# A chunked delta-rule recurrence: two pairs of small matmul groups issued alternately, and output heads in exchanged partition halves

## The chip, the cores and the metric

The kernel runs on one core of one Trainium2 chip. The metric is the device time of one execution in microseconds (us). Engines are named as in the profile: PE is TensorE (matmul), DVE is VectorE, ACT is ScalarE, POOL is GpSimd, SP issues DMAs.

## The reference

The model is a trunk of two layers over 1024 tokens of width 1024, in float32. Layer 0 mixes with a gated MLP and a pooling, layer 1 with the RWKV-7 time mixing; each is followed by a SwiGLU feed-forward part. The change touches the time mixing of layer 1 alone. Its core is this recurrence over tokens, for 16 heads with a state of 64 x 64 each:

```
def step(state, inp):
    r_t, w_t, k_t, v_t, a_t, b_t = inp
    sa = jnp.einsum('bhvk,bhk->bhv', state, a_t)
    state = (state * w_t[:, :, None, :] + sa[..., None] * b_t[:, :, None, :]
             + v_t[..., None] * k_t[:, :, None, :])
    return state, jnp.einsum('bhvk,bhk->bhv', state, r_t)
...
mean = jnp.mean(y, axis=-1, keepdims=True)
var = jnp.mean(jnp.square(y - mean), axis=-1, keepdims=True)
y = ((y - mean) * lax.rsqrt(var + GN_EPS)).reshape(bsz, seq, d)
y = y * ln_w.astype(f32) + ln_b.astype(f32)
bonus = jnp.sum(rh * kh * r_k.astype(f32), axis=-1, keepdims=True) * vh
y = (y + bonus.reshape(bsz, seq, d)).astype(h.dtype)
return (y * g) @ w_o, v_first
```

The kernel does not step token by token. It takes chunks of 64 tokens and solves each chunk with matrix products: with decayed a, b, k, r it forms all products inside the chunk, inverts a unit triangular 64 x 64 matrix, and carries the state only from chunk to chunk.

## The kernel before

The 1024 tokens are processed in two halves of 512, so there are eight chunks in each half and sixteen in all. Earlier stages write what a chunk needs to DRAM: `ar_d` (decayed a and r), `bk_d` (b and k), `v_d`, and `xi_d` (inverses of the 32 x 32 diagonal blocks of the triangular matrix). The function `recur` then runs the chunks of a half. It is a generator: `drive` interleaves its steps with those of a dense feed-forward stream (`ffn`), whose products are 128 x 128 x 512 and fill TensorE. The numbers that the generators yield are weights for that interleaving: small ones (0.1) inside a burst, and `BURST` = 12.0 between bursts.

Sixteen heads lie as eight pairs `p` with two members `r`: member r of a pair has its 64 rows in partitions 0 to 63 (r = 0) or 64 to 127 (r = 1). A product of 64 x 64 so uses one quarter of the 128 x 128 array: the operands' partition half picks the rows, the result's partition half picks the columns. All small products go through the helper `mm` (line 1460 is the call that the profile names for each), which chains them in program order with `issue_after`; dense products are placed between them by the tile planner, which simulates a timeline and gives the recurrence's instructions a priority ahead of the dense ones.

One chunk is one `burst` (line 1561), which issues, in this order:

- `below2` (line 1537): the lower left block of the inverse, 16 products of 32 x 32, copied into `XT` by ScalarE (r = 0) and VectorE (r = 1);
- `own` (line 1550): ov = the chunk's own values through its strictly lower products, copied from PSUM by ScalarE into `akv`. Its products read one partition half and write the other;
- oq: the state seen through a (`ar[..., 0, :]` with `S0`), products that read and write the same half; VectorE adds `akv` and oq into `Q` (line 1570);
- `gram` of the next chunk, first half: 16 products over all four quarters, masked from PSUM into `gt` by two VectorE multiplications (line 1507);
- ou: the solve, the inverse `XT` applied to `Q`; copied into `uv` by ScalarE (half 0, line 1577) and VectorE (half 1, line 1578);
- the output's state term (line 1587): r (`ar[..., 1, :]`) with `S0` into the PSUM tile `yp`;
- `gram` of the next chunk, second half; the state update (line 1597) with two VectorE operations; the output's own term, added into `yp` (line 1606); then `flip_bk` (transposes of the next chunk's b and k), loads by DMA for the chunk after next, and `below` (line 1521).

`yp` has two banks of PSUM, one per chunk of a pair of chunks. After the second chunk of a pair `post` (line 1632) copies both into `ysb` with ScalarE, normalises each head (VectorE, GpSimd), applies the weight `lnw`, adds the bonus term (`vch` times `bon`), and leaves `turn_out` (line 1678) to transpose the result and multiply it by the gate during the next burst. `lnw`, `vch` and `bon` are loaded by DMAs on SP's queue.

PSUM has eight banks. In these stages (`MIXED`, line 391) three go to the dense products, three to the small products (`sm`), two to `yp`.

Of the kernel before, what the change touches and what calls it, by code (L numbers as in the profile page):

```python
# [16 lines left out]
P = 128  # L17
# [26 lines left out]
def tile_trunk(  # L44
# [346 lines left out]
    MIXED = {"mm": ("mm", 3), "aux": ("sm", 3), "sm": ("sm", 3)}  # L391
# [792 lines left out]
    def project(h, hn1, kp, ring, keep, before_v):  # L1184
# [181 lines left out]
        for r in range(2):  # L1366
            sp.dma_start(
                bon[rows[r], h * 8 : h * 8 + 8, :], bon_d[h][:, :, r, :].rearrange("j (c t) p -> t (j c) p", t=64)
            )
# [70 lines left out]
    def recur(h, wp, stream):  # L1440
# [12 lines left out]
        C, ypair, loaded = {}, {}, [None]  # L1453
# [41 lines left out]
        def gram(c, q):  # L1495
            ar, bk, _, gt, _, _ = C[c]
            og = [pst("sm").rearrange("p (a b) -> p a b", b=P) for _ in range(2)]
            for j in range(4):
                p = q * 4 + j
                for b in range(2):  # L1500
                    for r in range(2):
                        mm(
                            og[r][rows[b], j, :], bk[rows[r], p, b, :],
                            ar[rows[r], p].rearrange("p a b -> p (a b)"), start=True, stop=True,
                        )
# [31 lines left out]
        def below2(c, w1):  # L1537
            XT = C[c][5]
            ox = smt()
            for p in range(8):  # L1540
                for r in range(2):
# [8 lines left out]
        def own(c):  # L1550

            _, _, uv, gt, _, _ = C[c]
            ov = smt()
# [3 lines left out]
            akv = wt("akv", 1, [P, 8, 64])  # L1557
            act.activation(akv, ov, AF.Copy)
            return akv

        def burst(c, bkt, w1):
# [4 lines left out]
            akv = own(c)  # L1566
            oq = smt()
            each(oq, lambda r, p: ar[rows[r], p, 0, :], lambda r, p: S0[rows[r], p, :])
            Q = wt("Q", 1, [P, 8, 64])
            dve.tensor_tensor(out=Q, in0=akv, in1=oq, op=ALU.add)  # L1570
# [5 lines left out]
            each(ou, lambda r, p: XT[rows[r], p, :], lambda r, p: Q[rows[r], p, :])  # L1576
            act.activation(uv[rows[0], 0], ou[rows[0]], AF.Copy)
            dve.tensor_copy(uv[rows[1], 1], ou[rows[1]])
            yield 0.1
            if c % 2 == 0:  # L1580
                ypair[0] = psum["pool"].tile([P, 2, 8, 64], F32, tag="y", bufs=1, name="yp")

            yp = ypair[0][:, c % 2]
            for p in range(8):
                for r in range(2):
                    mm(
                        yp[rows[r], p, :], ar[rows[r], p, 1, :], S0[rows[r], p, :], start=p == 0, stop=False,
                        skip_group_check=True,
                    )
# [13 lines left out]
            for p in range(8):  # L1603
                for r in range(2):
                    mm(
                        yp[rows[r], p, :], gt[:, p, r, 64:128], uv[:, r, p, :], start=False, stop=p == 7,
                        skip_group_check=True,
                    )
            C.pop(c)
            yield 0.1  # L1610
            if more:
# [5 lines left out]
                if c == 0:  # L1617
                    with tc.issue_after(loaded[0].ins):
                        for r in range(2):
                            i = sp.dma_start(  # L1620
                                lnw[rows[r]],
# [10 lines left out]
        def post(jj):  # L1632
            ysb = wt("ysb", 1, [P, 2, 8, 64])
            for r in range(2):
                act.activation(ysb[:, r], ypair[0][:, r], AF.Copy)
# [3 lines left out]
            with tc.issue_after(loaded[1].ins):  # L1639
                sp.dma_start(gch, g_d[h][:, :, jj * P : (jj + 1) * P])  # L1640
                for r in range(2):
                    sp.dma_start(
                        vch[rows[r]].rearrange("t c p d -> t c (p d)"),
# [6 lines left out]
            for r in range(2):  # L1650
                for p in range(8):
                    dve.bn_stats(out=st[:, r, p, :], in_=ysb[:, r, p, :])
# [13 lines left out]
            for p in range(8):  # L1666
                act.activation(
                    ysb[:, 1, p, :], ysb[:, 1, p, :], AF.Identity, scale=var[:, 8 + p : 9 + p], bias=mean[:, 8 + p : 9 + p]
                )
            dve.tensor_tensor(out=ysb[:, 0], in0=ysb[:, 0], in1=vb, op=ALU.mult)  # L1670
            dve.tensor_tensor(out=ysb[:, 0], in0=ysb[:, 0], in1=mb, op=ALU.add)
            yield 0.3
            for q in range(2):
                dve.tensor_tensor(out=ysb[:, q], in0=ysb[:, q], in1=lnw, op=ALU.mult)
                dve.tensor_tensor(out=ysb[:, q], in0=ysb[:, q], in1=vch[:, q], op=ALU.add)
            yield 0.3

            def turn_out():
                for q in range(2):
                    o = pst("sm")  # L1680
                    for i in range(4):
# [3 lines left out]
                            ysb[:, i % 2, p : p + 2, :].rearrange("t p d -> t (p d)"), ident,  # L1685
                        )
                    ov = o.rearrange("p (q c r t) -> p q r c t", q=2, c=2, r=2)
                    for i in range(4):
# [3 lines left out]
                            out=g, in0=ov[:, i // 2, i % 2], scalar=col(C_LNB + m), in1=g, op0=ALU.add, op1=ALU.mult,  # L1692
# [345 lines left out]
```

## Time and profile before

| | us |
|---|---|
| median of 3 timed runs (lowest 2453.6, highest 2456.31) | 2454.44 |
| span of the profiled execution | 2450.8 |
| first small product of the recurrence, first half | 1060.5 |
| last, second half (a transpose of `turn_out`) | 1834.4 |

The profiled execution's own time is known by its span alone, first to last instruction; the timed runs include what lies around it. In the views below a line gives the start in us, the duration, the engine, the line of the kernel, the operation, what it writes and reads by the program's tile names, the shape, and how many were merged (x); in brackets stands how long the engine was idle before and what released it. A view of waits gives us in total, times, and the longest. A stretch gives for each engine busy us and instructions, then the granted clock, the DMA engines' share and GB/s.

### The profile page before, as it was taken

The page shows a single profiled execution, that of the slowest core. Times are in us where ns is not written, and L with a number is a line of the kernel's source. Part 1 is how long each engine was busy: PE and PEld are TensorE (multiplying, and loading weights), DVE is VectorE, ACT ScalarE, POOL GpSimd, SP SyncE. Part 2 cuts the span into 40 slices and gives each one's busy share as a digit, 9 for nine tenths or more (in the row PEclk, how much of TensorE's full clock was granted, in tenths as well). Part 3 has the DMA queues.
Part 4 walks back from the last instruction along what each step waited for, and adds up shares of the span by engine and source line. Part 5 has one row for each costly group of instructions (what it writes and reads, how often), then busy time and mean ns, then how long its engine had stood idle before and what let it go on. Part 6 is the DMA issues. An engine that isn't in the chain of part 4 may idle for free. (4 is left out here: it accounts for less than half of the span.)

```text
span 2450.8 us, 38190 instructions
## 1 busy us (share of the span) xinstructions
PE 2369.0 (97%) x15567; PEld 1945.9 (79%) x15567; DVE 1476.8 (60%) x2328; ACT 935.9 (38%) x1403; POOL 217.1 (9%) x246
## 2 busy tenths in 40 slices
PE   8999999999899999999999999999999999999998
PEld 6888888888687788778777678777888788888887
DVE  6445766655558758856767947856664446434443
ACT  6233444443114644422335744433232324322223
POOL 0200000000000033101100133201100001000001
PEclk9999999999999999999999999999999999999999
DMA  5114443334655554774435465675433422433231
GB/s 177 52 60 140 153 146 103 113 103 155 252 203 204 165 149 131 226 212 132 129 126 155 160 166 141 186 223 158 143 112 122 129 78 90 150 105 95 86 103 52
DMA packets 406767, 342.17 MB, mean 140 GB/s; under 512 B 78080, under 2 KB 351616, under 8 KB 405824
## 3 DMA queue, kind: packets, MB, share of 16 engines
q10 hardware_dynamic: 266048, 195.33, 26.3%
q1 hardware_dynamic: 140544, 144.41, 18.8%
q8 instruction: 122, 2.00, 0.3%
q14 instruction: 53, 0.43, 0.0%
HBM read 263.07 MB, written 76.61 MB: 139 GB/s over the span
## 5 line engine op out<-in xcount | busy, mean ns | idle before, releaser
L399 PE MATMUL mm<-ahi,whi 128*128 128x512 f32 x1376 | 541.0, 394 | 5.8 <-DVE h L493 3.7
L400 PE MATMUL mm<-alo,whi 128*128 128x512 f32 x1376 | 541.5, 394 | 1.1 <-DVE alo L158 1.1
L401 PE MATMUL mm<-ahi,wlo 128*128 128x512 f32 x1376 | 540.1, 393 | 1.4 <-DVE wlo L158 1.4
L157 ACT ACTIVATE whi<-raw 128x1024 fp32r<-128x1024 f32 (+1 forms) x280 | 282.0, 1013 | 557.4 <-PE mm L400 428.6
L158 DVE TENSOR_TENSOR wlo<-raw,whi 128x1024 fp32r<-128x1024 f32 (+1 forms) x280 | 328.4, 1177 | 246.5 <-ACT whi L157 231.0
L399 PEld LDWEIGHTS mm<-ahi,whi 128*128 128x128 f32 x1376 | 259.0, 188 | 63.1 <-ACT whi L157 6.2
L401 PEld LDWEIGHTS mm<-ahi,wlo 128*128 128x128 f32 x1376 | 259.2, 188 | 58.4 <-DVE wlo L158 2.7
L400 PEld LDWEIGHTS mm<-alo,whi 128*128 128x128 f32 x1376 | 259.3, 188 | 57.7 <-issue 2.5
L493 DVE TENSOR_TENSOR h<-h,mm 128x512 f32<-128x512 f32 x276 | 185.5, 684 | 162.5 <-PE mm L401 161.6
L399 PE MATMUL mm<-hidhi,wdhi 128*128 128x512 f32 x304 | 117.5, 395 | 2.9 <-ACT hidhi L958 2.3
L400 PE MATMUL mm<-hidlo,wdhi 128*128 128x512 f32 x304 | 119.7, 394 | 0.0
L401 PE MATMUL mm<-hidhi,wdlo 128*128 128x512 f32 x304 | 119.0, 391 | 0.0
L730 PE MATMUL mm<-ahi,whi 128*128 128x512 f32 x296 | 115.6, 390 | 0.0
L731 PE MATMUL mm<-alo,whi 128*128 128x512 f32 x296 | 115.2, 389 | 0.0
L732 PE MATMUL mm<-ahi,wlo 128*128 128x512 f32 x296 | 113.6, 389 | 0.0
L157 ACT ACTIVATE wdhi<-raw 128x1024 fp32r<-128x1024 f32 x42 | 43.5, 1058 | 168.0 <-PE mm L400 133.1
L955 DVE TENSOR_TENSOR sg<-sg,mm 128x512 f32<-128x512 f32 x52 | 35.7, 687 | 118.9 <-PE mm L401 118.7
L399 PE MATMUL mm<-hd,dhi 128*128 128x512 f32 x192 | 75.8, 396 | 13.8 <-DMA hd<-hid_d 10.8
L400 PE MATMUL mm<-hd,dhi 128*128 128x512 f32 x192 | 75.9, 395 | 0.0
L401 PE MATMUL mm<-hd,dlo 128*128 128x512 f32 x192 | 74.8, 393 | 0.0
L399 PEld LDWEIGHTS mm<-hidhi,wdhi 128*128 128x128 f32 x304 | 57.3, 189 | 16.0 <-ACT hidhi L958 2.7
L401 PEld LDWEIGHTS mm<-hidhi,wdlo 128*128 128x128 f32 x304 | 57.5, 189 | 11.9
(395 smaller groups left out, 4278.2 us busy)
## 6 DMA issues: line engine op xcount, KB each, us to landing
raw<-in_ffn_w_down_dram ACTq DMA_DIRECT2D x88, 512.0 KB
raw<-in_ffn_w_gate_dram ACTq DMA_DIRECT2D x74, 512.0 KB
raw<-in_ffn_w_up_dram ACTq DMA_DIRECT2D x74, 512.0 KB
hid_d<-hid SPq DMA_DIRECT2D x36, 512.0 KB
hd<-hid_d SPq DMA_DIRECT2D x26, 512.0 KB
raw<-in_ab_w_in_dram ACTq DMA_DIRECT2D x16, 512.0 KB
raw<-in_ab_w_out_dram ACTq DMA_DIRECT2D x16, 512.0 KB
raw<-in_rwkv_w_r_dram ACTq DMA_DIRECT2D x16, 512.0 KB
```

The costliest lines, as they stand in the source:

```text
L157: act.activation(hi, src, AF.Copy)
L158: (eng or dve).tensor_tensor(out=lo, in0=src, in1=hi.bitcast(F32), op=ALU.subtract)
L399: pe.matmul(o, whi, xhi, start=first, stop=False)
L400: pe.matmul(o, whi, xlo, start=False, stop=False)
L401: pe.matmul(o, wlo, xhi, start=False, stop=last)
L493: dve.tensor_tensor(out=H[h][:, m, :], in0=H[h][:, m, :], in1=o, op=ALU.add)
L730: pe.matmul(o, wh[:, k, :], x[0][:, k, :], start=st, stop=False, skip_group_check=True)
L731: pe.matmul(o, wh[:, k, :], x[1][:, k, :], start=False, stop=False, skip_group_check=True)
L732: pe.matmul(o, wl[:, k, :], x[0][:, k, :], start=False, stop=k == 3, skip_group_check=True)
L955: dve.tensor_tensor(out=s, in0=s, in1=o, op=ALU.mult)
```

## The change

Own and oq become one group: `own` now takes the state, allocates both PSUM tiles and issues for each pair and member one product of ov and one of oq in turn. `akv` is gone; ScalarE copies ov straight into `Q`, and VectorE adds oq to it. The solve and the output's state term become one group as well, alternating product by product. So that these two fall on different quarters, the output of a head is written to the other partition half (`yp[rows[1 - r]]`), and everything that meets it there (`lnw`, `vch`, `bon`, the order in `turn_out`) is exchanged too. `yp` is one bank, copied into an `ysb` tile (three buffers) at the end of every chunk, and the bank that this leaves goes to `sm`, which has four. `gram` and `below2` take r = 1 before r = 0.

```diff
@@ -388,7 +388,7 @@
 
     FULL = {"mm": ("mm", 8)}
     DENSE = {"mm": ("mm", 5), "aux": ("aux", 3)}
-    MIXED = {"mm": ("mm", 3), "aux": ("sm", 3), "sm": ("sm", 3)}
+    MIXED = {"mm": ("mm", 3), "aux": ("sm", 4), "sm": ("sm", 4)}
     PROJ = {"mm": ("mm", 3), "aux": ("aux", 4), "bo": ("bo", 1)}
     ps_es = open_psum("psd0", DENSE)
 
@@ -1365,7 +1365,7 @@
         sp.dma_start(bon_d[h].rearrange("j t r p -> t j (r p)"), bs.rearrange("t j r p -> t j (r p)"))
         for r in range(2):
             sp.dma_start(
-                bon[rows[r], h * 8 : h * 8 + 8, :], bon_d[h][:, :, r, :].rearrange("j (c t) p -> t (j c) p", t=64)
+                bon[rows[1 - r], h * 8 : h * 8 + 8, :], bon_d[h][:, :, r, :].rearrange("j (c t) p -> t (j c) p", t=64)
             )
 
         xs = []
@@ -1450,7 +1450,7 @@
             return pst("sm").rearrange("p (a b) -> p a b", b=64)
 
         lnw = wt("lnw", 1, [P, 8, 64])
-        C, ypair, loaded = {}, {}, [None]
+        C, ypair, loaded = {}, [], [None]
         S, Q, last = [state_d], {}, []
 
         def ordered(f, *args, **kw):
@@ -1498,7 +1498,7 @@
             for j in range(4):
                 p = q * 4 + j
                 for b in range(2):
-                    for r in range(2):
+                    for r in (1, 0):
                         mm(
                             og[r][rows[b], j, :], bk[rows[r], p, b, :],
                             ar[rows[r], p].rearrange("p a b -> p (a b)"), start=True, stop=True,
@@ -1538,7 +1538,7 @@
             XT = C[c][5]
             ox = smt()
             for p in range(8):
-                for r in range(2):
+                for r in (1, 0):
                     b0 = r * 64
                     mm(
                         ox[b0 : b0 + 32, p, 0:32], w1[b0 + 32 : b0 + 64, p, :], XT[b0 + 32 : b0 + 64, p, 32:64],
@@ -1547,46 +1547,40 @@
             act.activation(XT[0:32, :, 32:64], ox[0:32, :, 0:32], AF.Copy)
             dve.tensor_copy(XT[64:96, :, 32:64], ox[64:96, :, 0:32])
 
-        def own(c):
-
-            _, _, uv, gt, _, _ = C[c]
-            ov = smt()
+        def own(c, S0):
+
+            ar, _, uv, gt, _, _ = C[c]
+            ov, oq = smt(), smt()
             for p in range(8):
                 for r in range(2):
                     mm(ov[rows[r], p, :], gt[rows[1 - r], p, r, 0:64], uv[rows[1 - r], r, p, :], start=True, stop=True)
-            akv = wt("akv", 1, [P, 8, 64])
-            act.activation(akv, ov, AF.Copy)
-            return akv
+                    mm(oq[rows[r], p, :], ar[rows[r], p, 0, :], S0[rows[r], p, :], start=True, stop=True)
+            Q = wt("Q", 1, [P, 8, 64])
+            act.activation(Q, ov, AF.Copy)
+            dve.tensor_tensor(out=Q, in0=Q, in1=oq, op=ALU.add)
+            return Q
 
         def burst(c, bkt, w1):
 
             ar, _, uv, gt, _, XT = C[c]
             cg, S0, more = h * 8 + c, S[0], c < 7
             below2(c, w1)
-            akv = own(c)
-            oq = smt()
-            each(oq, lambda r, p: ar[rows[r], p, 0, :], lambda r, p: S0[rows[r], p, :])
-            Q = wt("Q", 1, [P, 8, 64])
-            dve.tensor_tensor(out=Q, in0=akv, in1=oq, op=ALU.add)
+            Q = own(c, S0)
             yield 0.1
             if more:
                 gram(c + 1, 0)
                 yield 0.1
             ou = smt()
-            each(ou, lambda r, p: XT[rows[r], p, :], lambda r, p: Q[rows[r], p, :])
+            yp = psum["pool"].tile([P, 8, 64], F32, tag="y", bufs=1, name="yp")
+            for p in range(8):
+                for r in range(2):
+                    mm(ou[rows[r], p, :], XT[rows[r], p, :], Q[rows[r], p, :], start=True, stop=True)
+                    mm(
+                        yp[rows[1 - r], p, :], ar[rows[r], p, 1, :], S0[rows[r], p, :], start=p == 0, stop=False,
+                        skip_group_check=True,
+                    )
             act.activation(uv[rows[0], 0], ou[rows[0]], AF.Copy)
             dve.tensor_copy(uv[rows[1], 1], ou[rows[1]])
-            yield 0.1
-            if c % 2 == 0:
-                ypair[0] = psum["pool"].tile([P, 2, 8, 64], F32, tag="y", bufs=1, name="yp")
-
-            yp = ypair[0][:, c % 2]
-            for p in range(8):
-                for r in range(2):
-                    mm(
-                        yp[rows[r], p, :], ar[rows[r], p, 1, :], S0[rows[r], p, :], start=p == 0, stop=False,
-                        skip_group_check=True,
-                    )
             yield 0.1
             if more:
                 gram(c + 1, 1)
@@ -1603,9 +1597,12 @@
             for p in range(8):
                 for r in range(2):
                     mm(
-                        yp[rows[r], p, :], gt[:, p, r, 64:128], uv[:, r, p, :], start=False, stop=p == 7,
+                        yp[rows[1 - r], p, :], gt[:, p, r, 64:128], uv[:, r, p, :], start=False, stop=p == 7,
                         skip_group_check=True,
                     )
+            ysb = wt("ysb", 3, [P, 8, 64])
+            act.activation(ysb, yp, AF.Copy)
+            ypair.append(ysb)
             C.pop(c)
             yield 0.1
             if more:
@@ -1618,7 +1615,7 @@
                     with tc.issue_after(loaded[0].ins):
                         for r in range(2):
                             i = sp.dma_start(
-                                lnw[rows[r]],
+                                lnw[rows[1 - r]],
                                 rwkv_ln_w[0].rearrange("(p r d) -> r p d", r=2, d=64)[r].partition_broadcast(64),
                             )
                     loaded.append(i)
@@ -1630,9 +1627,7 @@
         turned = []
 
         def post(jj):
-            ysb = wt("ysb", 1, [P, 2, 8, 64])
-            for r in range(2):
-                act.activation(ysb[:, r], ypair[0][:, r], AF.Copy)
+            ysb = [ypair.pop(0) for _ in range(2)]
             j = h * 4 + jj
             gch = wt("gch", 1, [P, 8, P])
             vch = wt("vch", 1, [P, 2, 8, 64])
@@ -1640,7 +1635,7 @@
                 sp.dma_start(gch, g_d[h][:, :, jj * P : (jj + 1) * P])
                 for r in range(2):
                     sp.dma_start(
-                        vch[rows[r]].rearrange("t c p d -> t c (p d)"),
+                        vch[rows[1 - r]].rearrange("t c p d -> t c (p d)"),
                         v_d[h][jj * P : (jj + 1) * P, r].rearrange("(c t) p d -> t c (p d)", t=64),
                     )
             v16 = vch.rearrange("t c p d -> t (c p) d")
...
@@ -1682,14 +1677,14 @@
                         p = 4 * q + i // 2 * 2
                         ordered(
                             pe.transpose, o[:, i * P : (i + 1) * P],
-                            ysb[:, i % 2, p : p + 2, :].rearrange("t p d -> t (p d)"), ident,
+                            ysb[i % 2][:, p : p + 2, :].rearrange("t p d -> t (p d)"), ident,
                         )
                     ov = o.rearrange("p (q c r t) -> p q r c t", q=2, c=2, r=2)
                     for i in range(4):
                         m = q * 4 + i
                         g = gch[:, m, :].rearrange("p (c t) -> p c t", c=2)
                         dve.scalar_tensor_tensor(
-                            out=g, in0=ov[:, i // 2, i % 2], scalar=col(C_LNB + m), in1=g, op0=ALU.add, op1=ALU.mult,
+                            out=g, in0=ov[:, i // 2, 1 - i % 2], scalar=col(C_LNB + m), in1=g, op0=ALU.add, op1=ALU.mult,
                         )
                 sp.dma_start(y_d[h][:, :, jj * P : (jj + 1) * P], gch)
```

The hunks cut here change `ysb[:, q]` to `ysb[q]` in the normalisation and nothing else.

More of the change, by code (lines that the diff above doesn't have):

```diff
@@ L1651, in post @@
                 for p in range(8):
-                    dve.bn_stats(out=st[:, r, p, :], in_=ysb[:, r, p, :])
+                    dve.bn_stats(out=st[:, r, p, :], in_=ysb[r][:, p, :])
             sts = st.rearrange("p a b s -> p (a b) s")
@@ L1667, in post @@
                 act.activation(
-                    ysb[:, 1, p, :], ysb[:, 1, p, :], AF.Identity, scale=var[:, 8 + p : 9 + p], bias=mean[:, 8 + p : 9 + p]
+                    ysb[1][:, p, :], ysb[1][:, p, :], AF.Identity, scale=var[:, 8 + p : 9 + p], bias=mean[:, 8 + p : 9 + p]
                 )
-            dve.tensor_tensor(out=ysb[:, 0], in0=ysb[:, 0], in1=vb, op=ALU.mult)
-            dve.tensor_tensor(out=ysb[:, 0], in0=ysb[:, 0], in1=mb, op=ALU.add)
+            dve.tensor_tensor(out=ysb[0], in0=ysb[0], in1=vb, op=ALU.mult)
+            dve.tensor_tensor(out=ysb[0], in0=ysb[0], in1=mb, op=ALU.add)
             yield 0.3
             for q in range(2):
-                dve.tensor_tensor(out=ysb[:, q], in0=ysb[:, q], in1=lnw, op=ALU.mult)
-                dve.tensor_tensor(out=ysb[:, q], in0=ysb[:, q], in1=vch[:, q], op=ALU.add)
+                dve.tensor_tensor(out=ysb[q], in0=ysb[q], in1=lnw, op=ALU.mult)
+                dve.tensor_tensor(out=ysb[q], in0=ysb[q], in1=vch[:, q], op=ALU.add)
             yield 0.3
```

## The prediction

> **What bounds the kernel now.** I read the busy times by stretch first, to see which engine fills the two recurrences (the stretches 1060 to 1260 us and 1640 to 1835 us of a span of 2450.8 us):
>
> ```profile
> span 2450.8 us, 38190 instructions
> ...
> core 0: us, PE busy (x) PEld busy (x) DVE busy (x) ACT busy (x) POOL busy (x), PEclk, DMA share, GB/s
> ...
> 1060.00:1260.00 200.00, 189.47 (x3073) 158.09 (x3071) 126.90 (x272) 63.36 (x118) 23.79 (x20) 0.99 0.49 144
> ...
> 1640.00:1835.00 195.00, 189.71 (x2996) 159.03 (x2996) 121.27 (x264) 64.67 (x119) 23.79 (x20) 0.99 0.46 132
> ```
>
> TensorE is busy 189.5 of 200 and 189.7 of 195 us, VectorE some 63%, ScalarE a third, the granted clock is 0.99. Dense feed-forward products fill what the recurrence leaves free, so time that the recurrence gives back on TensorE is time that the span loses, unless it turns into a wait. Next, TensorE's timeline of one clean burst (chunk 5 of the first half). The helper `mm` is line 1460 and records every small product there, so I tell them by tiles: XT,w is `below2`, uv,gt is `own` (ov), S,ar into sm is oq, ar,bk is `gram`, Q,XT is ou, S,ar into yp the state term of the output, uv,bkt the state update. Each of these float32 products shows as two matmul records, so 16 products are 32.
>
> ```profile
> 1188.45 0.69 PE L1460 MATMUL sm<-XT,w 32*32 32x32 f32 x30
> 1189.06 0.97 PE L1460 MATMUL sm<-uv,gt 64*64 64x64 f32 x26
> ...
> 1189.93 0.22 PE L1460 MATMUL sm<-S,ar 64*64 64x64 f32 x1
> 1189.94 0.22 PE L1460 MATMUL sm<-uv,gt 64*64 64x64 f32 x1
> 1189.94 0.22 PE L1460 MATMUL sm<-S,ar 64*64 64x64 f32 x1
> 1189.99 0.22 PE L1460 MATMUL sm<-uv,gt 64*64 64x64 f32 x1
> 1189.99 0.22 PE L1460 MATMUL sm<-S,ar 64*64 64x64 f32 x1
> 1189.99 0.22 PE L1460 MATMUL sm<-uv,gt 64*64 64x64 f32 x1
> 1190.00 0.98 PE L1460 MATMUL sm<-S,ar 64*64 64x64 f32 x27
> 1190.81 0.38 PE L1460 MATMUL sm<-ar,bk 64*64 64x128 f32 x2
> 1191.12 0.50 PE L401 MATMUL mm<-ahi,wlo 128*128 128x512 f32 x1
> ...
> 1192.95 0.99 PE L1460 MATMUL sm<-ar,bk 64*64 64x128 f32 x27
> ...
> 1193.79 1.01 PE L1460 MATMUL sm<-Q,XT 64*64 64x64 f32 x27
> ...
> 1194.76 0.22 PE L1460 MATMUL sm<-Q,XT 64*64 64x64 f32 x1
> ...
> 1195.72 1.07 PE L1460 MATMUL sm<-ar,bk 64*64 64x128 f32 x29
> 1196.72 1.15 PE L1460 MATMUL sm<-uv,bkt 128*64 128x64 f32 x32
> ```
>
> Three things are to be seen. A product of 64 rows by 64 columns uses a quarter of the array. Own uses the quarters that cross from one partition half to the other, oq the two that stay in their half; each alone runs at 0.81/27 = 0.030 us per record (S,ar, 1190.00 to 1190.81), a pair per 0.06 us. At the seam, where own's last and oq's first overlap, the records start four at a time: four at 1189.93 to 1189.94, four at 1189.99 to 1190.00. So two quarters stand idle for all of own, oq, ou and yp. And gram, which already issues all four quarters in turn, gets records of 128 columns through at (1193.79 - 1192.95)/30 = 0.028 us, the pace at which the two-quarter groups pass 64 columns. Lastly, an island of seven dense products lies inside the first gram (1191.12 to 1192.95), long enough for what happens on ScalarE and VectorE:
>
> ```profile
> 1190.26 0.60 ACT L1558 ACTIVATE akv<-sm 128x512 f32<-128x512 f32 x1 [0.71 <-PE sm L1460]
> ...
> 1191.09 0.69 DVE L1570 TENSOR_TENSOR Q<-akv,sm 128x512 f32<-128x512 f32 x1 [1.09 <-PE sm L1460]
> ...
> 1195.02 0.59 ACT L1577 ACTIVATE uv<-sm 64x512 f32<-64x512 f32 x1 [4.16 <-PE sm L1460]
> ...
> 1195.64 0.69 DVE L1578 COPY uv<-sm 64x512 f32<-64x512 f32 x1 [0.26 <-ACT uv L1577]
> ```
>
> Q is ready at 1191.78, and ou starts only some 1.9 us later. After ou it is tight: uv's second half is copied only when ScalarE has done the first (VectorE idle 0.26, released by ACT uv), ready at 1196.33, and the state update starts at 1196.72. What TensorE waits for in the two stretches:
>
> ```profile
> PE sm L1460 <- DVE gt L1507: 3.0, 6, 1.0
> ...
> PE sm L1460 <- DMA bk<-bk_d: 2.2, 1, 2.2
> ...
> PE sm L1460 <- ACT akv L1558: 0.5, 1, 0.5
> ...
> PE sm L1460 <- DMA bk<-bk_d: 2.0, 1, 2.0
> PE sm L1460 <- DVE gt L1507: 2.0, 4, 1.3
> PE sm L1460 <- ACT akv L1558: 1.3, 1, 1.3
> ```
>
> **The change, part by part.** No matmul is added or taken away: in each of 16 chunks 64 records of own and oq, and 64 of ou and yp, are reordered.
>
> *Own with oq.* Before, 1189.06 to 1190.81 = 1.75 us. At the seam's pace 64 records are 16 groups of 0.06 = 0.96, with a start like own's some 1.0: 0.75 saved. Bounds of a pace that the trace never shows for a whole group: below, the seam; above, the slowest group that alternates without a wait and has less work per record, XT,w with 0.61/30 = 0.020 us, 64 of them 1.3 us. I take the seam, since gram holds four quarters over a whole group with twice the columns. A rule speaks against it. The Trainium skill's TensorEngine Tiling (Array Packing), Restrictions and Gotchas, says that different row tiles can't use one PSUM bank at the same time; the new order has both halves write both banks, and by the rule nothing would overlap, for which the sum is in the last rival but one. The trace disagrees: own alone writes one tile from both halves at 0.030 per record, and the eight records of the seam write two tiles from both.
>
> Q's chain gets longer, since ScalarE now copies ov after both groups. From own's start: 1.0 of products, 0.22 of the last record, 0.05 to the copy's start, 0.60, 0.05, VectorE's addition 0.69: Q stands at 2.6, against 2.72 before (1191.78 - 1189.06). It is no later, but the first gram is done by 1.0 + 0.95, so dense work has to cover 0.66 us. Cover is there, the island of 1.83 us; it moves from inside gram to ahead of ou. If it doesn't come, 0.66 is lost per chunk and the island's own cost, 1.83 - 7 x 0.23 = 0.2, is saved. Queued behind a late Q are ou, yp, the second gram and the state update, on TensorE and in that order. Two bursts start gram late because bk has not landed (2.2 and 2.0 us); there the 0.75 only lengthens that wait. So 14 x 0.75 = 10.5 us.
>
> *Ou with yp.* Before, 1193.79 to 1195.72 = 1.93 us, now 1.0: 0.93 less on TensorE. But yp and the second gram were the cover for the copies of uv. Ou's last record starts at 1194.76; uv is ready 1.57 later, the state update 1.96 later. The new pair ends about when ou alone did, and behind it stand only the second gram (1.0, with the switch 1.2). The state update then starts 1.62 after, and 0.34 is what remains: the rest is a new wait of 0.4 us for VectorE's copy. Five bursts are late already, on the masks of the first gram:
>
> ```profile
> 1169.31 2.35 DVE L158 TENSOR_TENSOR wlo<-raw,whi 128x1024 fp32r<-128x1024 f32 x2
> ...
> 1171.58 1.28 DVE L1507 TENSOR_TENSOR gt<-sm,gm 128x512 f32<-128x512 f32 x2
> ...
> 1172.32 0.43 PE L1460 MATMUL sm<-ar,bk 64*64 64x128 f32 x2 [1.00 <-DVE gt L1507]
> 1172.89 0.69 DVE L1578 COPY uv<-sm 64x512 f32<-64x512 f32 x1
> ...
> 1173.94 0.45 PE L1460 MATMUL sm<-uv,bkt 128*64 128x64 f32 x8
> ```
>
> VectorE is in weight splits until 1171.66, and uv is copied by 1173.58 however fast TensorE gets there: 0.3 is gained there. So 11 x 0.34 + 5 x 0.3 = 5.2 us; bounds, nothing and 16 x 0.93 = 14.9 (dense work put into the gap).
>
> *A fourth small PSUM buffer, from the output's second bank.* The first gram no longer needs the buffer that the copy of ov gives free: the two waits for akv, 0.5 + 1.3 = 1.8 us, go. The waits for gt (3.0 and 2.0) stay, as the second gram's first tile still falls on one of the first gram's.
>
> *At nothing.* The output's copies stay 16 of ScalarE's 0.6 us kind, one in each chunk where two came in every second; they run beside the transposes of bk, and ScalarE sat idle 4.16 us in this burst alone. If that cover went, the even chunks' copy would hold up bk's by 0.6, 8 x 0.6 = 4.8 us at most, and the odd chunks' would come that much earlier. Dropping akv and holding three half outputs takes the same room. The exchanged halves change targets of DMAs on SP (bon, lnw, vch), none in number or size, and their place in SP's queue stays. The order of r in gram and below2 moves no work between engines. One step less of 0.1 in the interleaving is nothing beside the burst's 12.
>
> **Sum.** 10.5 + 5.2 + 1.8 = 17.5 us off the profiled execution's span, 2450.8 to 2433.3. The three timed runs have a median of 2454.44, 3.6 more than the span, which I add: 2437.
>
> **The rivals.**
>
> *All of it arrives.* The planner fills the new wait before the state update: 16 x (0.75 + 0.93) + 1.8 = 28.7, 2426. For it: it did put seven dense products where it saw a wait. Against: the wait for gt in five bursts shows that it misses some.
>
> *Little arrives.* No island before Q: 14 x (0.75 - 0.66 + 0.2) = 4.1, with 5.2 and 1.8 11 us, 2443. Or the pace is XT,w's, 1.3 us a group: own saves 14 x 0.45 = 6.3, ou nothing, with 1.8 8 us, 2446.
>
> *The pace stalls near 0.025 us.* A group of 64 takes y; own gains 1.75 - y; the state update comes y + 1.62 after ou's start against 0.97 + 1.96 = 2.93, so ou gains 1.31 - y. With 0.11 per chunk from akv it is nought at y = 1.58, 0.025 us a record; the time is then 2454 to 2455. Of the same pace is the Trainium skill's TensorE: Matmul & The Clock Gate, Wait — 56ns, not 53.3ns?, with a floor of about 25 ns between starts; XT,w at 0.020 over 30 records speaks against it here.
>
> *No overlap, slower.* The four kinds run in order, two quarters at a time: own with oq 1.75 to 1.92 as before, ou with yp 1.92, and uv can only be copied when both are done: 1.92 + 1.62 = 3.54 against 2.93, a loss of 0.6 per chunk. 16 x 0.6 - 1.8 = +8, 2462. It decides from a pace above 0.025. The seam and gram speak against it.
>
> *VectorE in front, slower.* The planner sets a pair of splits (2.35 us) ahead of both Q's addition and gt. The island leaves 1.83 - 0.66 = 1.17 for Q, so 1.18 is lost there; at gt the 1.00 + 0.17 of today grow by 0.93: 3.3 per burst. From 17.5/3.3 = 5 more bursts of 16 it eats the gain; at eight it is +9, 2463. The five late bursts speak for it, VectorE's 63% against.
>
> **How the numbers follow.** Forecast 0.48 (2437), all 0.18 (2426), little 0.14 (2443 to 2446), stalled pace 0.10 (2455), no overlap 0.05 (2462), VectorE in front 0.05 (2463). The first three make 0.80 and lie within 2424 to 2450, with 2 us below for placement and 4 above. About 0.2% (5 us) is what a measurement here can tell from no change. Faster by more 0.80, the same 0.10, slower 0.10.
>
> **What would show it.** In TensorE's timeline uv,gt and S,ar alternate, with some 1.0 us from own's start to gram's or the island's; above 1.3 the pace is wrong. A dense island ahead of Q,XT, or else a wait for DVE Q of about 0.7. A wait or gap ahead of uv,bkt of 0.4 us, released by DVE uv: without it all arrives. No waits for the copy of ov at gram. The forecast is wrong if own and oq still take 1.7, if DVE gt's waits grow past some 10 us, or if time moves outside the two stretches.

## The result and the profile after

The changed kernel takes 2433.6 us (median of four runs, 2427.72 to 2435.55), the kernel before 2455.38 beside it (four runs). The ratio is 0.9898 with a 95% interval of 0.9879 to 0.9918, so the change saves 20 to 30 us by the interval and 21.8 by the medians. The profiled span fell by 19.7, from 2450.8 to 2431.1 us. The head of the page after:

```profile
span 2431.1 us, 38203 instructions
...
PE 2347.3 (97%) x15567; PEld 1917.3 (79%) x15567; DVE 1475.1 (61%) x2328; ACT 937.1 (39%) x1403; POOL 214.8 (9%) x246
```

TensorE does the same 15567 matmul records in less busy time; before, this row began with 2369.0, which is 21.7 more. The stretches of the two recurrences after, with the columns of the prediction's table:

```profile
1060.00:1260.00 200.00, 189.52 (x3119) 152.27 (x3118) 133.35 (x282) 65.04 (x119) 23.12 (x20) 0.98 0.52 147
1620.00:1815.00 195.00, 189.22 (x3072) 154.04 (x3065) 126.03 (x269) 67.61 (x122) 22.93 (x20) 0.99 0.54 152
```

TensorE is as busy as it was (189.5 and 189.7), but 46 and 76 more records pass in the same 200 and 195 us. Counted by their starts, 46 and 45 of these are dense products; the rest of the second stretch's are small ones, since it cuts the recurrence at another place. So the time was not turned into idling; dense products took it. TensorE's, ScalarE's and VectorE's timeline of the same burst as in the prediction (chunk 5):

```profile
1185.95 0.69 PE L1460 MATMUL sm<-XT,w 32*32 32x32 f32 x32
1186.58 0.27 PE L1460 MATMUL sm<-uv,gt 64*64 64x64 f32 x1
1186.58 0.27 PE L1460 MATMUL sm<-S,ar 64*64 64x64 f32 x1
1186.59 0.27 PE L1460 MATMUL sm<-uv,gt 64*64 64x64 f32 x1
1186.60 0.27 PE L1460 MATMUL sm<-S,ar 64*64 64x64 f32 x1
1186.68 0.22 PE L1460 MATMUL sm<-uv,gt 64*64 64x64 f32 x1
...
1187.52 0.22 PE L1460 MATMUL sm<-S,ar 64*64 64x64 f32 x1
1187.56 1.12 PE L1460 MATMUL sm<-ar,bk 64*64 64x128 f32 x32
1187.79 0.60 ACT L1559 ACTIVATE Q<-sm 128x512 f32<-128x512 f32 x1 [0.72 <-PE sm L1460]
1188.42 0.69 DVE L1560 TENSOR_TENSOR Q<-Q,sm 128x512 f32<-128x512 f32 x1 [0.90 <-ACT Q L1559]
1188.61 0.50 PE L399 MATMUL mm<-ahi,whi 128*128 128x512 f32 x1
...
1190.10 0.39 PE L399 MATMUL mm<-hidhi,whi 128*128 128x512 f32 x1
1190.41 0.27 PE L1460 MATMUL sm<-Q,XT 64*64 64x64 f32 x1
1190.42 0.27 PE L1460 MATMUL yp<-S,ar 64*64 64x64 f32 x1
...
1191.60 1.04 PE L1460 MATMUL sm<-ar,bk 64*64 64x128 f32 x30
1192.57 0.50 PE L400 MATMUL mm<-hidlo,whi 128*128 128x512 f32 x1
1192.89 0.59 ACT L1582 ACTIVATE uv<-sm 64x512 f32<-64x512 f32 x1 [1.24 <-PE sm L1460]
1193.52 0.70 DVE L1583 COPY uv<-sm 64x512 f32<-64x512 f32 x1 [0.53 <-ACT uv L1582]
1193.53 0.33 PE L1460 MATMUL sm<-uv,bkt 128*64 128x64 f32 x2 [0.23 <-ACT uv L1582]
1193.79 0.50 PE L399 MATMUL mm<-hidhi,whi 128*128 128x512 f32 x1
...
1195.05 0.39 PE L401 MATMUL mm<-hidhi,wlo 128*128 128x512 f32 x1
1195.37 1.09 PE L1460 MATMUL sm<-uv,bkt 128*64 128x64 f32 x29
```

Four records start at 1186.58 to 1186.60, two of each kind, which is one for each quarter. Own with oq takes 0.98 us to gram's start (1186.58 to 1187.56) where it took 1.75. Over all 16 chunks the distance from the first to the last of its 64 records fell from 1.69 to 0.94; for ou with yp, from 1.83 to 2.15 down to 0.94 in twelve chunks and 1.08 to 1.13 in four. The island of dense products has moved: it now stands between the first gram and ou (1188.61 to 1190.41), and Q is ready at 1189.11 behind it. Two dense products, of which 1192.57 is the first, stand where the copy of uv would be waited for, and six more (1193.79 to 1195.05) stand inside the state update, after its first two records.

What TensorE waits for in the recurrences, over the whole execution:

```profile
PE sm L1460 <- DMA bk<-bk_d: 8.8, 4, 6.0
...
PE sm L1460 <- DVE gt L1507: 2.9, 2, 1.6
...
PE sm L1462 <- DMA bk<-bk_d: 2.1, 1, 2.1
PE sm L1460 <- DVE Q L1560: 1.7, 2, 1.3
...
PE sm L1460 <- DVE XT L1548: 1.1, 2, 0.8
...
PE sm L1460 <- ACT uv L1582: 0.9, 3, 0.4
...
PE sm L1460 <- DVE uv L1583: 0.2, 1, 0.2
```

That is 17.7 us together, against 16.0 before. The waits for akv (1.8) are gone, and so is one of 2.8 for the copy of bkt, which the prediction did not name; the wait for gt is smaller (2.9 against 5.0). But the wait for bk's load grew from 6.4 to 10.9, and the waits for Q, XT and uv, 3.9 together, are new.

Where the 19.7 us lie can be counted. From the length of each recurrence (first to last small product) I take off 0.2275 us, the pace at which dense products start one behind another, for each 512-column product that starts inside. Before, 201.6 - 425 x 0.2275 = 104.9 and 208.0 - 476 x 0.2275 = 99.7; after, 198.9 - 461 x 0.2275 = 94.1 and 199.3 - 494 x 0.2275 = 86.9. The recurrences' own cost fell from 204.6 to 181.0, by 23.6. Counted in the same way, the time ahead of the first recurrence grew by 1.6, the stretch between the two by 1.8, and the rest by 0.4. The two pairs of groups alone give 16 x 0.75 = 12.0 and 31.4 - 15.7 = 15.7, together 27.7; some 4 of it were given back inside the recurrences, bk's 4.5 among them.

### The profile page after: what moved, and what is told of

Same layout as the page of the kernel before. It is cut to its first block, busy times and chain, and to the rows that moved or that the text cites. A ratio compares the mean times of both kernels' runs of the same rounds, so it can differ in the third digit from the quotient of the medians.

```text
span 2431.1 us, 38203 instructions
## 1 busy us (share of the span) xinstructions
PE 2347.3 (97%) x15567; PEld 1917.3 (79%) x15567; DVE 1475.1 (61%) x2328; ACT 937.1 (39%) x1403; POOL 214.8 (9%) x246
## 5 line engine op out<-in xcount | busy, mean ns | idle before, releaser
L399 PE MATMUL mm<-hd,dhi 128*128 128x512 f32 x192 | 75.9, 396 | 13.8 <-DMA hd<-hid_d 11.4
L400 PEld LDWEIGHTS mm<-hidlo,wdhi 128*128 128x128 f32 x304 | 57.9, 190 | 12.3 <-issue 0.5
```

The source lines that it names most:

```text
L399: pe.matmul(o, whi, xhi, start=first, stop=False)
L400: pe.matmul(o, whi, xlo, start=False, stop=False)
```

## The experiments

"Own cost" below is the recurrences' own cost as just counted: 204.6 before, 181.0 after. Each kernel was timed against the kernel before on its own chip (medians of that one from 2454.32 to 2455.96).

**One pair alone.** The kernel before, with only own and oq alternated: no exchanged halves, no fourth buffer.

```diff
                     mm(ov[rows[r], p, :], gt[rows[1 - r], p, r, 0:64], uv[rows[1 - r], r, p, :], start=True, stop=True)
+                    mm(oq[rows[r], p, :], ar[rows[r], p, 0, :], S0[rows[r], p, :], start=True, stop=True)
...
-            oq = smt()
-            each(oq, lambda r, p: ar[rows[r], p, 0, :], lambda r, p: S0[rows[r], p, :])
```

> Edit: the kernel before with own and oq issued alternately and nothing else (akv kept, three small buffers, ou and yp apart in the same halves). Theory 'four quarters': 64 records of own and oq take 1.0 us instead of 1.75 in each chunk, ou and yp stay at some 1.9; the time falls by 8 to 12 us, to 2443 to 2447. Rival 'placement and buffers' (the gain comes from the fourth buffer, the earlier copies and where the planner puts dense products): no gain, 2452 to 2458.

Measured: 2449.72 (2443.54 to 2455.11), ratio 0.9977 (0.9965 to 0.9989). Own with oq takes 0.94 in this kernel too. Its own cost is 191.6, or 13 lower than before, but 7.3 came back in the stretch between the recurrences. So the pace is a matter of the order alone; 12 us of products were worth 5 in the time, less than the 8 to 12 that were expected.

**No alternation.** The changed kernel with both pairs issued one group after the other.

```diff
-                    mm(oq[rows[r], p, :], ar[rows[r], p, 0, :], S0[rows[r], p, :], start=True, stop=True)
+            each(oq, lambda r, p: ar[rows[r], p, 0, :], lambda r, p: S0[rows[r], p, :])
...
-                    mm(ou[rows[r], p, :], XT[rows[r], p, :], Q[rows[r], p, :], start=True, stop=True)
+            each(ou, lambda r, p: XT[rows[r], p, :], lambda r, p: Q[rows[r], p, :])
+            for p in range(8):
+                for r in range(2):
                     mm(
                         yp[rows[1 - r], p, :], ar[rows[r], p, 1, :], S0[rows[r], p, :], start=p == 0, stop=False,
```

> Edit: the changed kernel with both pairs issued one after the other again (all of ov, then all of oq; all of ou, then all of yp); fourth buffer, exchanged halves, a copy per chunk and the order of r stay. Four quarters: own with oq back to 1.7 to 1.8 us, ou with yp to 1.8 to 1.9; the time returns to 2452 to 2460. Placement and buffers: the time stays within 5 us of the changed kernel, 2430 to 2440.

Measured: 2462.65 (2457.98 to 2468.26), ratio 1.0031 (1.0021 to 1.004). TensorE's timeline:

```profile
1202.85 0.92 PE L1460 MATMUL sm<-Q,XT 64*64 64x64 f32 x26
...
1203.73 0.92 PE L1460 MATMUL yp<-S,ar 64*64 64x64 f32 x25
...
1204.54 1.04 PE L1460 MATMUL sm<-ar,bk 64*64 64x128 f32 x30
```

The time is above the expected range. Ou and yp stand one behind the other again, 1.69 us for both. Everything else of the change, without the alternation, is 8 us slower than before. Against the changed kernel 29 us are lost: some 24 in the two pairs, and TensorE's waits in the recurrences are 30.5 us here against 17.7. The whole gain hangs on the alternation.

**Same halves.** The changed kernel with the output's heads left in their own halves: ou and yp still alternate, but on the same two quarters.

```diff
-                        yp[rows[1 - r], p, :], ar[rows[r], p, 1, :], S0[rows[r], p, :], start=p == 0, stop=False,
+                        yp[rows[r], p, :], ar[rows[r], p, 1, :], S0[rows[r], p, :], start=p == 0, stop=False,
```

The second term of yp, `lnw`, `vch`, `bon` and the order in `turn_out` follow.

> Edit: the changed kernel with the output heads back in their own partition halves, so that ou and yp alternate in the same two quarters. Four quarters: ou with yp takes 1.9 us again, own with oq 1.0; 16 x 0.9 lost, 2444 to 2449. Placement and buffers: as the changed kernel, 2430 to 2438.

Measured: 2448.69 (2444.19 to 2450.39), ratio 0.9972 (0.9958 to 0.9986). TensorE's timeline of ou and yp:

```profile
1191.05 0.34 PE L1460 MATMUL sm<-Q,XT 64*64 64x64 f32 x4
1191.21 0.29 PE L1460 MATMUL yp<-S,ar 64*64 64x64 f32 x4
1191.33 0.33 PE L1460 MATMUL sm<-Q,XT 64*64 64x64 f32 x4
1191.45 0.33 PE L1460 MATMUL yp<-S,ar 64*64 64x64 f32 x4
```

Four records in 0.12 us, 0.03 each: the two-quarter pace, 1.91 for the group, while own with oq stays at 0.94 in 15 of 16 chunks. Over all chunks ou with yp takes 30.5 us against 15.7, 14.8 more. The medians differ by 15.1 us and the own cost by 14.2 (195.2); the profiled spans differ by 11.4, this one being the fastest of its six executions. Dense products start in the same numbers as in the changed kernel, 461 and 494 in the recurrences and 1256 between them, so the planner's placement hardly differs between these two. Nearly the whole of what ou and yp save on TensorE arrives in the time, and it is the exchanged halves that save it.

**Three small buffers.** The changed kernel with `sm` back at three banks; the eighth bank lies idle.

```diff
-    MIXED = {"mm": ("mm", 3), "aux": ("sm", 4), "sm": ("sm", 4)}
+    MIXED = {"mm": ("mm", 3), "aux": ("sm", 3), "sm": ("sm", 3)}
```

> Edit: the changed kernel with three buffers for the small products instead of four, the freed bank unused. Four quarters: both groups keep 1.0 us; waits for the copy of ov or for masks come back, 2 to 6 us, 2435 to 2441. Placement and buffers: most of the gain goes, 2446 or more.

Measured: 2456.06 (2450.99 to 2460.01), ratio 1.0001 (0.9989 to 1.0014): with three buffers the whole gain is gone, although own with oq takes 0.94 in every chunk and ou with yp 0.89 to 1.08. The waits:

```profile
PE sm L1460 <- DVE XT L1548: 7.4, 4, 3.1
...
PE sm L1460 <- DVE gt L1507: 3.4, 15, 1.1
PE sm L1460 <- DVE ysb L1670: 3.2, 2, 2.9
```

Of the 18.2 us by which the span exceeds the changed kernel's, the recurrences have 9.2 (own cost 190.2). Gram now waits for a mask in fifteen places, and for `below2`'s copy and the transposes of the output in others; but the waits grow by 3.7 us only (21.4 against 17.7), and what makes up the rest is not traced. The stretch between the recurrences, in which none of their small products run, has 11.9. It begins at 1275 here and at 1261 in the changed kernel. The profile from 1260 to 1320, first here and then in the changed kernel:

```profile
1260.00:1280.00 20.00, 13.57 (x61) 10.66 (x59) 17.73 (x36) 7.94 (x17) 3.79 (x3) 0.88 0.31 114
1280.00:1300.00 20.00, 9.66 (x22) 5.48 (x23) 17.45 (x25) 11.61 (x17) 0.35 (x1) 0.67 0.79 254
1300.00:1320.00 20.00, 18.25 (x68) 14.37 (x68) 11.30 (x15) 9.10 (x13) 0.00 (x0) 0.85 0.57 159
```

```profile
1260.00:1280.00 20.00, 17.09 (x70) 12.69 (x69) 16.02 (x27) 8.64 (x12) 0.20 (x1) 0.91 0.70 215
1280.00:1300.00 20.00, 16.91 (x73) 12.57 (x72) 8.57 (x10) 5.82 (x6) 1.01 (x1) 1.00 0.69 192
1300.00:1320.00 20.00, 19.21 (x83) 15.23 (x82) 18.91 (x28) 13.70 (x21) 0.00 (x0) 1.00 0.52 172
```

Behind a recurrence that has drawn in more dense products (509 and 617 against 461 and 494), TensorE has 151 records here where the changed kernel has 226, and a granted clock down to 0.67; in the 60 us from the end of each one's recurrence it has 167 and 224. The clock in these traces is either full or half. Over the whole stretch half-clock time is 41.0 us against 10.2. That suggested that the price of the missing buffer is a lack of dense work behind the recurrence. Two pairs of runs were to tell.

**More dense work held back, by the interleaving's ratio.** The edit of both kernels, with three and with four buffers:

```diff
-RATIO, AHEAD, INV, FINE = 3.0, 450, 5, 1
+RATIO, AHEAD, INV, FINE = 3.5, 450, 5, 1
...
-    drive(ffn(0, 1, nxt["hn"], f, D0P[:3], nd=2), recur(0, wp, in_pieces(hb_pool, 1, h_d[1, 0])), 6.2)
+    drive(ffn(0, 1, nxt["hn"], f, D0P[:3], nd=2), recur(0, wp, in_pieces(hb_pool, 1, h_d[1, 0])), 7.0)
```

> Edit: three small buffers as in e4, and the recurrence advanced faster against the dense stream (interleaving ratios 6.2 to 7.0 and 3.0 to 3.5). Theory 'tail': with three buffers the recurrence ends too late beside a dense stream that runs out, TensorE idles and its clock is halved after it; ahead in time, that part comes back: 8 to 13 us less than with three buffers, 2443 to 2448. Rival 'burst waits': the loss lies in the waits inside the bursts, which stay: 2453 to 2460.

> Edit: the changed kernel with the same two ratios (7.0 and 3.5), as a control. Tail: its recurrence already ends in time, so little changes, 2430 to 2438. Rival: any earlier recurrence gains as much as with three buffers, 2421 to 2427.

Measured: 2458.08 (2451.16 to 2462.77), ratio 1.001 (0.9997 to 1.0022), and 2434.12 (2429.83 to 2440.03), ratio 0.992 (0.9901 to 0.9939). The number of dense products inside the recurrences is the same as without the edit (509 and 617; 461 and 494), so the edit moved none of them, and the pair tests nothing. It does show what the same work gives twice: 2456.06 and 2458.08, 2433.6 and 2434.12.

**More dense work held back, by moving it.** 48 dense products are taken from the work ahead of the first recurrence and given to the list that runs behind it; the edit is made with three buffers, and with four.

```diff
-    D0B = [[a, a + 1, a + 2] for a in range(f, f + 12, 3)], [[a, a + 1] for a in range(f + 12, 22, 2)]
+    D0B = [[f, f + 1, f + 2], [f + 3, f + 4, f + 5], [f + 6, f + 7], [f + 8, f + 9]], [[a, a + 1] for a in range(f + 10, 22, 2)]
...
-    prime_b, steps_b = down_steps(1, D0B[1], lambda f: whl(), hslot, True, spill_h, (next(between[0]) for _ in range(4)))
+    prime_b, steps_b = down_steps(1, D0B[1], lambda f: whl(), hslot, False, spill_h, (next(between[0]) for _ in range(4)))
```

> Edit: three small buffers as in e4, and 48 dense products of the feed-forward part of layer 0 (two hidden blocks of the down product) moved from ahead of the first recurrence to behind it. Theory 'tail': behind a recurrence that ends late the dense stream runs out, the norm of the next half waits uncovered, and the clock is halved; with 48 products (10.9 us) more behind it the stretch between the two recurrences loses its excess (84 us over the dense products' own time with three buffers, 72 in the changed kernel): 8 to 12 us less than e4, 2444 to 2449. Rival 'burst waits': no gain, 2453 to 2460.

> Edit: the changed kernel with the same 48 products moved, as a control. Tail: its first recurrence already ends in time, nothing to gain, 2430 to 2438. Rival (any cover behind the recurrence gains): 2420 to 2427.

Measured: 2455.08 (2453.09 to 2457.23), ratio 1.0006 (0.9997 to 1.0015), and 2444.82 (2441.05 to 2446.79), ratio 0.9964 (0.9951 to 0.9976). With three buffers 36 of the 48 went beside the first recurrence (545 against 509) and only 12 behind it. The stretch between cost 4.1 less, the part ahead 5.1 more, and half-clock time in between was still 30.7. So the theory was met only by a quarter of its dose, and it gained nothing. With four buffers the move costs 11 us: 85 more dense products stood behind the first recurrence there (1341 against 1256), and the stretch still cost 4 us more. It is not shown that a lack of dense work is the cause.

A count does tie the loss to the granted clock. At half clock dense products start every 0.43 us instead of 0.23 (with three buffers, 1290.15 to 1291.86 for four steps), so a microsecond of it costs a busy TensorE about half. With half of its half-clock time taken off, the stretch between the recurrences costs 63.4 us before (13.7 at half clock), 63.5 with three buffers and 66.9 in the changed kernel; over all fourteen kernels it is 60.5 to 67.8, where the cost itself runs from 69.0 to 85.6. The kernel with the earlier transposes below, which has four buffers, has 31.2 us at half clock there. So, by this count, the 12 us go with the clock behind the first recurrence and not with the buffer as such. Why some orders leave TensorE idle there, and others less, stays open.

**The order inside the state update.** The island of six products inside the state update stands between a product that needs ScalarE's half of uv and one that needs VectorE's. The changed kernel with the other order:

```diff
-                each(os_, lambda r, p: bkt[:, p, r * 64 : r * 64 + 64], lambda r, p: uv[:, r, p, :])
+                for p in range(8):
+                    for r in (1, 0):
+                        mm(os_[rows[r], p, :], bkt[:, p, r * 64 : r * 64 + 64], uv[:, r, p, :], start=True, stop=True)
```

> Edit: the changed kernel, with r = 1 before r = 0 in the state update, which needs the copy of uv that VectorE makes last. In the changed kernel's timeline two records of the update start on ScalarE's half, and six dense products are set between them and the rest. Theory 'split island': one island of eight takes the place of two, some 0.4 us less in 14 chunks, 3 to 6 us faster than the changed kernel, 2427 to 2431. Rival (the island's two switches cost nothing, since the dense products are wanted anyway): no difference, 2432 to 2436.

Measured: 2442.71 (2437.3 to 2445.2), ratio 0.9944 (0.9927 to 0.9961), 9 us slower than the changed kernel. The state update did get shorter (its records keep TensorE busy for 17.9 us in all, against 22.1), but the planner placed other work differently: TensorE's waits in the recurrences are 29.3 us against 17.7, most of the growth at gt. In the second recurrence:

```profile
PE sm L1460 <- DVE gt L1507: 9.3, 3, 7.0
```

The 3 to 6 us that the theory promised did not come. Since other waits moved by more than that, the run does not show that the split costs nothing.

**Earlier transposes.** In the changed kernel the transposes of the next bk come ahead of the state update, so that small products cover uv's copy; `bkt` becomes two half tiles with three buffers.

```diff
                 gram(c + 1, 1)
                 yield 0.1
+                second = flip_bk(c + 1)
+                yield 0.1
...
-                bkt = flip_bk(c + 1)
+                bkt = second()
```

> Edit: the changed kernel, with the next chunk's transposes of b and k issued ahead of the state update instead of at the burst's end (bkt in halves, three buffers; the second half is copied after the update). They take 1.0 us on TensorE, more than the 0.4 us by which uv is late. Theory 'cover': the two islands ahead of the update go, 0.6 to 0.9 us in 14 chunks, and bk's buffer comes free earlier, so that the waits for bk (10.9 us) shrink: 2418 to 2428. Rival: the transposes only move, and the copies of bkt or the masks end last instead: 2432 to 2438.

The same with the moved dense work of the pair above:

> Edit: e6 (transposes ahead of the state update) with the same 48 products moved. In e6 the two recurrences cost 175 us beside the dense products against 181 in the changed kernel, but the stretch between them 80 against 72. Tail: the 8 us come back, 2426 to 2430, faster than the changed kernel. Rival: 2433 to 2438, as e6.

Measured: 2435.71 (2432.94 to 2436.97), ratio 0.9917 (0.9902 to 0.9932), and 2436.19 (2430.62 to 2442.81), ratio 0.9931 (0.9911 to 0.9951). In the first the own cost falls by another 6 us, to 174.9, and the stretch between takes 7.6 more; one wait there, in the part that follows a recurrence, is

```profile
PE aux L434 <- DVE nacc L413: 6.4, 1, 6.4
```

The second shows neither gain (own cost 180.9; its profiled execution is the longest of its four). Neither beats the changed kernel.

**Alternating in blocks.** The changed kernel with both pairs alternating by two head pairs: eight records of the one kind, then eight of the other.

```diff
-            for p in range(8):
-                for r in range(2):
-                    mm(ov[rows[r], p, :], gt[rows[1 - r], p, r, 0:64], uv[rows[1 - r], r, p, :], start=True, stop=True)
-                    mm(oq[rows[r], p, :], ar[rows[r], p, 0, :], S0[rows[r], p, :], start=True, stop=True)
+            for p0 in range(0, 8, 2):
+                for p in (p0, p0 + 1):
+                    for r in range(2):
+                        mm(ov[rows[r], p, :], gt[rows[1 - r], p, r, 0:64], uv[rows[1 - r], r, p, :], start=True, stop=True)
+                for p in (p0, p0 + 1):
+                    for r in range(2):
+                        mm(oq[rows[r], p, :], ar[rows[r], p, 0, :], S0[rows[r], p, :], start=True, stop=True)
```

Ou and yp in the same way.

> Edit: the changed kernel with both pairs alternating in blocks of two head pairs (eight records of the one, then eight of the other) instead of product by product. Theory 'queue looks ahead': TensorE takes records for idle quarters from several places further on, as at the seam of the kernel before, so a group of 64 still takes 1.0 to 1.1 us and the time stays, 2431 to 2437. Rival 'strict alternation': the groups take 1.3 us or more, 10 us or more slower, 2444 to 2452.

Measured: 2447.52 (2436.84 to 2453.59), ratio 0.9971 (0.9957 to 0.9985). Its timeline of ou and yp:

```profile
1209.36 0.27 PE L1460 MATMUL sm<-Q,XT 64*64 64x64 f32 x2
1209.39 0.27 PE L1460 MATMUL yp<-S,ar 64*64 64x64 f32 x2
1209.47 0.23 PE L1460 MATMUL sm<-Q,XT 64*64 64x64 f32 x2
1209.50 0.22 PE L1460 MATMUL yp<-S,ar 64*64 64x64 f32 x2
```

The records of the two kinds start beside each other although eight of one kind are issued before the other's first; own with oq takes 0.99 in every chunk. TensorE finds the idle quarters over a block of eight. And yet the kernel is 14 us slower than the changed one: its waits in the recurrences are 31.1 against 17.7, spread over bk's load (15.4), uv, XT and the state update's sum (which shares Q's buffer). An edit that TensorE hardly feels (0.05 a group) has moved the waits by 13 us. Not all of the 14 us need be the order: the ten executions of this one kernel spread from 2436.84 to 2453.59, with granted clocks from 0.980 to 0.989, and the profiled one (2453.44, 0.980) is among the longest.

## Why the prediction was right, and where its steps were not

The forecast was 17.5 us off the span and 2437; measured are 19.7 off the span and 2433.6. Direction, mechanism and size hold, the size in part by luck. Step by step:

- **Own with oq: right.** 1.0 us forecast, 0.98 in the burst shown, the same in all 16 chunks. Both rules of the Trainium skill that spoke for a slower pace disagree with the trace. Against the bank rule of the Trainium skill's TensorEngine Tiling (Array Packing), Restrictions and Gotchas, products from both row halves write each of the two tiles, in different partitions, at 15 ns a record. Against the floor of about 25 ns in the Trainium skill's TensorE: Matmul & The Clock Gate, Wait — 56ns, not 53.3ns?, the 64 records take 0.94 / 64 = 15 ns each.
- **Q's longer chain: right.** Q stands 2.53 us after own's start (1189.11 - 1186.58; forecast 2.6), and the island moved ahead of ou. Only two waits for Q are left, 1.7 us.
- **Ou with yp: the mechanism was right, the term mis-sized.** The second gram does end before uv is copied, as the prediction said: in five chunks the state update starts 1.69 us after the start of ou's last record, where before it started 1.96 after it in nine, while gram's own records end some 0.9 earlier. The step "the rest is a new wait of 0.4 us for VectorE's copy" failed: the planner set dense products there, and of the waits for uv only 1.1 us exist in the whole execution. So 0.34 x 11 + 0.3 x 5 = 5.2 was too little; the run with the same halves measured 15.1, the upper bound of the term (14.9) that the rival "all of it arrives" had taken. By the prediction's own sign, without that wait all arrives, 28.7 us. The two pairs did give 27.7 on TensorE, but 19.7 came off the span: 4 went again inside the recurrences and 4 outside.
- **VectorE's splits: no loss.** Of the five bursts that were late on the masks two are left; the waits for gt are 2.9 us in two places instead of 5.0 in ten, and the rival "VectorE in front" did not come about.
- **The fourth buffer: the sign was right, the size was not.** The step counted the waits for akv that would go, 1.8 us, and they went. Without the fourth buffer the kernel loses 22 us. A reason that the step left out, argued and not shown by itself, is that an alternating group takes two tiles at once, so that three buffers hold it up more than they held up the old order. In the profiled spans 9 of the loss lie in the recurrences, 3.7 of these as waits, and 12 in the stretch between, where they go with the half-clock time; what binds them to the buffer is open, since one test did not alter the order and the other gave only a quarter of its dose.
- **At nothing: not quite.** The wait for bk's load grew by 4.5 us (6.4 to 10.9), where the prediction had let two bursts lose their 0.75 each. This took back a part of what the terms above gave beyond the forecast; why the load came later is not shown.
- **The sum.** The terms as the runs with one edit give them (5.0 for own alone, 15.1 for the exchanged halves, 22.5 for the buffer) don't add up to 21.8. Most of these runs also carry a new placement of the dense products and other waits, which moved the time by 9 to 14 us in the reordering, block and moved-work runs. By a count, the granted clock carries much of that. With half of the half-clock time taken off the profiled spans, these are 2422.8 before and 2422.7 without alternation; 2411.4 with one pair alone and 2413.4 with the same halves; 2399.5 changed, 2400.6 reordered and 2403.8 in blocks. The steps then fit what the groups save (one pair 11.4 of 12.0, exchanged halves 13.9 of 14.8), and the reordering and the blocks lie hardly further off than the changed kernel with the other ratio, which has the same placement (2403.0). Three buffers (2410.1) and the moved work with four (2409.6) stay 10 us off. The count is from one execution each and no test, and it does not set the half-clock time apart from the waits. That the forecast came within 4 us owes something to errors that cancel: ou with yp and the buffer were put too low, and nothing was set against them for a longer wait for bk's load or for time outside the recurrences.

## What to carry to other kernels

Look at which quarters of the array a group of small products leaves idle, and issue beside it a group that uses just those; if both use the same, exchange the partition halves of one result where nothing downstream minds. Count the PSUM tiles that then live at once: here, without another buffer, the faster groups were worth nothing in the time. Where a planner fills the gaps, forecast the TensorE work that is saved and expect the new gap to be filled, but don't trust a single edit's time to better than the 9 to 14 us that a new placement, its waits and the granted clock moved here; look at the half-clock time of two runs before you explain their difference.

## What the runs showed of the hardware

- Float32 products of 64 x 64 on four quarters start in fours, 6 to 7 ns apart within a four, and 64 records pass in 0.94 us, 15 ns each. On two quarters it is 0.03 us a record, in the kernel before and in the run with the same halves alike.
- The four quarters needn't be named in turn: with blocks of eight records of one kind the 64 records took 0.99 us, so TensorE starts records of the second block while the first block's quarters are still busy. With 32 records of one kind ahead of 32 of the other it is 1.69 us.
- The granted clock fell to 0.67 in a stretch of 20 us in which TensorE was busy for 9.66 (three buffers, 1280 to 1300), and was 1.00 in the changed kernel's, busy for 16.91. Dense products start every 0.43 us at half clock and every 0.23 at full clock.
